# Residual layer norm: loads and stores through two on-chip rings of rows, a shorter pipeline, and one add in eight moved from TensorE to VectorE

## The chip, the cores and the metric

The kernel runs on one core of one Trainium2 chip. The metric is the device time of one execution in microseconds (us). The span of a profile, from the first to the last instruction, is 1.7 to 2.1 us shorter than the time of the same execution (3.2 us in one execution of dma_instr). Kernels are compared through their ratios to the kernel before (which was 251.4 to 251.7 us).

## The reference

```python
batch, seq, dim = 16, 1024, 512            # x and residual: float32, 33.5 MB each
z = x + residual
mean = np.mean(z, axis=-1, keepdims=True)
var = np.var(z, axis=-1, keepdims=True)
return (gamma * (z - mean) / np.sqrt(var + eps) + beta).astype(np.float32)
```

There are 16384 rows of 512 numbers. On the chip they are 128 "rows" j of 128x512 (one row per partition, 0.262 MB). For each, two inputs come in and one output goes out: 3 x 128 x 0.262 = 100.67 MB in all.

## The kernel before

Rows arrive in chunks of mostly 8, through two pools of buffers. TensorE adds z = x + residual into PSUM, the memory that its matmuls write, by two matmuls with the identity; ScalarE copies the sum back and totals it, then squares and totals; VectorE finishes. The stages of one group of 4 rows are spread over four steps.

```python
CHUNKS = [2, 2, 4] + [8] * 14 + [4, 2, 2]
GROUP = 4
STORE_LAG = 5          # in chunks
Z_BUFS = 7
R_BUFS = 4
# ... cut ...
    def g_add(g):                                   # TensorE
        # ... cut ...
        for j in range(j0, j0 + n):
            nc.tensor.matmul(ps, ident, Z[c][:, j, :], start=True, stop=False)
            nc.tensor.matmul(ps, ident, R[c][:, j, :], start=False, stop=True)
# ... cut: act_step = copy with a sum, square with a sum, sqrt (ScalarE);
#     affine1 = (z - mean) * gamma, affine2 = z * rstd + beta (VectorE, in place) ...
        for t in range(n_groups + 3):
            if ok(t) is not None:
                g_add(t)
            act_step(ok(t), ok(t - 1), ok(t - 2))   # copy t, square t-1, sqrt t-2
            if ok(t - 2) is not None:
                affine1(t - 2)
            if ok(t) is not None:
                negmean(t)
            if ok(t - 3) is not None:
                affine2(t - 3)
# ... cut ...
    for k in range(n_chunks + STORE_LAG):           # all on the sync engine's queue
        if k < n_chunks:
            load(k)
        c = k - STORE_LAG
        if c >= 0:
            while done <= c:
                done = next(steps)
            store(c)
```

## Time and profile before

| | before |
|---|---|
| time, median of 3 | 251.33 us (251.07 to 251.74) |
| span of the profile | 249.7 us |
| TensorE busy; its last matmul ends | 226.2 us; 229.3 us |
| VectorE busy; ends | 182.7 us; 246.0 us |
| DMA rate, 10 to 220 us | 428 GB/s |

Lines of the page of the kernel before: busy time of each engine, then the DMA engines' busy tenths and GB/s in 40 slices of 6.2 us, the DMA queues, and the chain of work that ended last, by engine.

```profile
PE 226.2 (91%) x516; PEld 99.2 (40%) x516; DVE 182.7 (73%) x328; ACT 180.4 (72%) x548; POOL 0.7 (0%) x6
...
DMA  6999999999999999999999999999999999987087
GB/s 245 421 440 428 425 429 379 438 427 425 436 430 430 429 433 425 428 433 433 428 428 430 425 433 425 433 425 433 428 432 427 428 430 416 427 353 299 42 357 315
...
q1 hardware_dynamic: 8640, 100.67, 95.4%
q8 instruction: 4, 0.07, 0.1%
q14 instruction: 8, 0.07, 0.1%
...
PE 88%; DVE 8%; DMA 1%; issue 1%; ACT 0%; DVEq 0%
```

The chain of waits is 88% TensorE, so TensorE looks like the limit. But the rate line stands between 416 and 440 GB/s in every slice from the 2nd to the 35th but one (379), so the DMA is full too. Both are close to their limit. The last five slices are what matters: 353, 299, 42, 357, 315.

The costliest groups (busy us, mean ns of one | idle us before) and the end in windows of 10 us (busy us and count per engine, granted TensorE clock, DMA share, GB/s):

```profile
L112 PE MATMUL ps<-z,ident 128*128 128x512 f32 x256 | 132.4, 599 | 0.0
...
L176 DVE SCALAR_TENSOR_TENSOR z<-z,nm,gamma_t 128x512 f32<-128x512 f32 x128 | 87.7, 745 | 1.1 <-ACT junk L139 1.1
```

```profile
core 0: us, PE busy (x) PEld busy (x) DVE busy (x) ACT busy (x) POOL busy (x), PEclk, DMA share, GB/s
...
210.00:220.00 10.00, 10.00 (x24) 4.39 (x24) 8.77 (x16) 8.66 (x29) 0.00 (x0) 1.00 1.03 433
220.00:230.00 10.00, 9.30 (x22) 3.80 (x20) 8.73 (x18) 8.66 (x27) 0.00 (x0) 1.00 0.68 287
230.00:240.00 10.00, 0.00 (x0) 0.00 (x0) 9.93 (x18) 4.98 (x17) 0.00 (x0) 0.68 0.37 157
240.00:250.00 10.00, 0.00 (x0) 0.00 (x0) 5.88 (x11) 0.00 (x0) 0.00 (x0) 0.50 0.82 341
```

A row has four matmul records (two matmuls, two records each) whose starts lie 0.43 us apart; 128 x 1.72 = 220 us. Up to 220 us the DMA share is 1. Then the loads are over, only stores of rows still being normalised are left, and the share falls to 0.68 and 0.37: the DMA engines wait for VectorE, which ends at 246.0 us.

### The profile page before, as it was taken

The page shows a single profiled execution, that of the slowest core. Times are in us where ns is not written, and L with a number is a line of the kernel's source. Part 1 is how long each engine was busy: PE and PEld are TensorE (multiplying, and loading weights), DVE is VectorE, ACT ScalarE, POOL GpSimd, SP SyncE. Part 2 cuts the span into 40 slices and gives each one's busy share as a digit, 9 for nine tenths or more (in the row PEclk, how much of TensorE's full clock was granted, in tenths as well). Part 3 has the DMA queues.
Part 4 walks back from the last instruction along what each step waited for, and adds up shares of the span by engine and source line. Part 5 has one row for each costly group of instructions (what it writes and reads, how often), then busy time and mean ns, then how long its engine had stood idle before and what let it go on. Part 6 is the DMA issues. An engine that isn't in the chain of part 4 may idle for free.

```text
span 249.7 us, 2117 instructions
## 1 busy us (share of the span) xinstructions
PE 226.2 (91%) x516; PEld 99.2 (40%) x516; DVE 182.7 (73%) x328; ACT 180.4 (72%) x548; POOL 0.7 (0%) x6
## 2 busy tenths in 40 slices
PE   5999999999999999999999999999999999997000
PEld 1444444444444444444444444444444444442000
DVE  1121266888888888898888888888988888889993
ACT  2157578888777777788887777777888877779600
POOL 1000000000000000000000000000000000000000
PEclk9999999999999999999999999999999999999755
DMA  6999999999999999999999999999999999987087
GB/s 245 421 440 428 425 429 379 438 427 425 436 430 430 429 433 425 428 433 433 428 428 430 425 433 425 433 425 433 428 432 427 428 430 416 427 353 299 42 357 315
DMA packets 8656, 100.80 MB, mean 404 GB/s; under 512 B 962, under 2 KB 962, under 8 KB 2500
## 3 DMA queue, kind: packets, MB, share of 16 engines
q1 hardware_dynamic: 8640, 100.67, 95.4%
q8 instruction: 4, 0.07, 0.1%
q14 instruction: 8, 0.07, 0.1%
q10 hardware_dynamic: 4, 0.00, 0.0%
HBM read 67.11 MB, written 33.55 MB: 403 GB/s over the span
## 4 chain that ended last, share of the span: by engine, by line
PE 88%; DVE 8%; DMA 1%; issue 1%; ACT 0%; DVEq 0%
PE ps L112 43%; PE ps L113 43%; DVE z L191 5%; DVE z L176 3%; PE ps L98 1%; DMA gb_row<-in_gamma_dram 1%; ACT z L121 0%; DVEq L267 0%; DVE rstd L188 0%; DVE nm L163 0%
## 5 line engine op out<-in xcount | busy, mean ns | idle before, releaser
L112 PE MATMUL ps<-z,ident 128*128 128x512 f32 x256 | 132.4, 599 | 0.0
L113 PE MATMUL ps<-r,ident 128*128 128x512 f32 x256 | 131.7, 596 | 0.0
L121 ACT ACTIVATE z<-ps 128x512 f32<-128x512 f32 x128 | 75.4, 589 | 50.2 <-PE ps L113 50.2
L139 ACT ACTIVATE junk<-z,nm 128x512 f32<-128x512 f32 x128 | 90.5, 711 | 1.4 <-DVE nm L163 1.4
L191 DVE SCALAR_TENSOR_TENSOR z<-z,rstd,beta_t 128x512 f32<-128x512 f32 x128 | 87.8, 747 | 1.2
L176 DVE SCALAR_TENSOR_TENSOR z<-z,nm,gamma_t 128x512 f32<-128x512 f32 x128 | 87.7, 745 | 1.1 <-ACT junk L139 1.1
L112 PEld LDWEIGHTS ps<-z,ident 128*128 128x128 f32 x256 | 49.1, 192 | 62.8 <-issue 48.7
L113 PEld LDWEIGHTS ps<-r,ident 128*128 128x128 f32 x256 | 49.0, 192 | 62.3 <-issue 61.7
L163 DVE TENSOR_SCALAR nm<-sm 128x4 f32<-128x4 f32 (+1 forms) x34 | 5.8, 170 | 54.9 <-ACT z L121 54.9
L121 ACT ACTIVATION_READ_ACCUMULATOR z<-ps 128x1 f32 x128 | 24.9, 195 | 0.0
L139 ACT ACTIVATION_READ_ACCUMULATOR junk<-z,nm 128x1 f32 x128 | 24.4, 191 | 0.0
L151 ACT ACTIVATE std<-ssq,eps_t 128x4 f32<-128x4 f32 (+1 forms) x34 | 9.8, 289 | 0.1
L98 PE MATMUL ps<-gb_row,ones 1*128 1x512 f32 x4 | 3.7, 1085 | 3.1 <-DMA gb_row<-in_gamma_dram 3.1
L188 DVE RECIPROCAL rstd<-std 128x4 f32<-128x4 f32 (+1 forms) x34 | 5.8, 170 | 0.0
L121 ACT ACT_TABLE_LOAD x1 | 1.3, 1283 | 4.3 <-DMA z<-in_x_dram 4.3
L99 DVE COPY gamma_t<-ps 128x512 f32<-128x512 f32 x1 | 0.7, 692 | 4.2 <-PE ps L98 4.2
L98 PEld LDWEIGHTS ps<-gb_row,ones 1*128 1x128 f32 x4 | 1.1, 307 | 4.2 <-issue 3.3
L99 DVE COPY beta_t<-ps 128x512 f32<-128x512 f32 x1 | 0.7, 692 | 1.0 <-PE ps L98 1.0
L151 ACT ACT_TABLE_LOAD x1 | 1.3, 1283 | 0.0
L87 DVE MEMSET ones<- 1x128 f32 x1 | 0.2, 165 | 0.8 <-PEq L253 0.8
masks.py:199 POOL TENSOR_SCALAR_AFFINE_SELECT ident<-ident 128x128 f32<-128x128 f32 x1 | 0.3, 295 | 0.1
masks.py:197 POOL MEMSET ident<- 128x128 f32 x1 | 0.2, 205 | 0.3 <-POOLq L253 0.3
(5 smaller groups left out, 0.5 us busy)
## 6 DMA issues: line engine op xcount, KB each, us to landing
z<-in_x_dram SPq DMA_DIRECT2D x14, 2048.0 KB, 19.4
r<-in_residual_dram SPq DMA_DIRECT2D x14, 2048.0 KB, 23.9
out_dram<-z SPq DMA_DIRECT2D x14, 2048.0 KB, 26.6
z<-in_x_dram SPq DMA_DIRECT2D x4, 512.0 KB, 7.4
r<-in_residual_dram SPq DMA_DIRECT2D x4, 512.0 KB, 8.2
z<-in_x_dram SPq DMA_DIRECT2D x2, 1024.0 KB, 9.0
r<-in_residual_dram SPq DMA_DIRECT2D x2, 1024.0 KB, 15.0
out_dram<-z SPq DMA_DIRECT2D x4, 512.0 KB, 8.3
```

Of the source, the lines that this page charges most:

```text
L87: nc.vector.memset(ones, 1.0)
L98: nc.tensor.matmul(ps, ones, gb_row[:, k, :], start=True, stop=True)
L99: nc.vector.tensor_copy(dest, ps)
L112: nc.tensor.matmul(ps, ident, Z[c][:, j, :], start=True, stop=False)
L113: nc.tensor.matmul(ps, ident, R[c][:, j, :], start=False, stop=True)
L121: nc.scalar.activation(out=Z[c][:, j0 + k, :], in_=PS[g_copy][k], func=ACT.Identity, accum_out=sm[:, k : k + 1],)
L139: nc.scalar.activation(out=junk, in_=Z[c][:, j0 + k, :], func=ACT.Square, bias=NM[g_square][:, k : k + 1], accum_out=ssq[:, k : k + 1],)
L151: nc.scalar.activation(out=std[:, :n], in_=SSQ.pop(g)[:, :n], func=ACT.Sqrt, bias=eps_t[:, 0:1], scale=inv_d,)
L163: nc.vector.tensor_scalar(out=nm[:, :n], in0=NM[g][:, :n], scalar1=-inv_d, scalar2=None, op0=ALU.mult,)
L176: nc.vector.scalar_tensor_tensor(out=zj, in0=zj, scalar=NM[g][:, k : k + 1], in1=gamma_t, op0=ALU.add, op1=ALU.mult,)
L188: nc.vector.reciprocal(out=rstd[:, :n], in_=STD.pop(g)[:, :n])
L191: nc.vector.scalar_tensor_tensor(out=zj, in0=zj, scalar=rstd[:, k : k + 1], in1=beta_t, op0=ALU.mult, op1=ALU.add,)
```

## The change

Its intent is to let loads run further ahead, to move larger pieces, to shorten the pipeline, and to take work off TensorE. The two pools become two rings of 64 and 32 rows; loads are 2 MB from the first one on (the last two of each input 1 MB); stores are 4 MB (the last three smaller), asked for when the loads are at least 40 rows ahead; every eighth row is added on VectorE; the pipeline has three steps. Below, R stands for the rings with their chunk sizes, P for the three-step pipeline, V for the vector adds.

```diff
-CHUNKS = [2, 2, 4] + [8] * 14 + [4, 2, 2]
+X_CHUNKS = [8] * 15 + [4, 4]
+R_CHUNKS = [8] * 15 + [4, 4]
+OUT_CHUNKS = [16] * 7 + [8, 4, 4]
 GROUP = 4
-STORE_LAG = 5
-Z_BUFS = 7
-R_BUFS = 4
+Z_ROWS = 64
+R_ROWS = 32
+STORE_LAG = 40
+ADD_PERIOD = 8
 # ... cut: pools replaced by two tiles addressed modulo their rows ...
+    def add_on_vector(g):
+        # ... cut ...
+        for j in range(j0, j0 + n):
+            if on_vector(j):                       # j % ADD_PERIOD == ADD_PERIOD - 1
+                nc.vector.scalar_tensor_tensor(
+                    out=zrow(j), in0=zrow(j), scalar=0.0, in1=rrow(j),
+                    op0=ALU.add, op1=ALU.add,
+                    accum_out=SM[g][:, j - j0 : j - j0 + 1])
 # ... cut ...
+        stages = [
+            (0, add),
+            (0, copy_then_sqrt),
+            (1, square),
+            (2, affine2),
+            (0, add_on_vector),
+            (1, affine1),
+            (0, negmean),
+        ]
+        for t in range(n_groups + 2):
 # ... cut ...
+    for lo, n in spans(X_CHUNKS):
+        asked = lo + n
+        load_x(lo, n)
+        while loads_r and loads_r[0][0] + loads_r[0][1] <= asked:
+            while added < loads_r[0][0] + loads_r[0][1] - R_ROWS:
+                added, done = next(steps)
+            load_r(*loads_r.pop(0))
+        store_due()        # stores whose rows end at or before asked - STORE_LAG
```

More of the change, by code (lines that the diff above doesn't have):

```diff
@@ L40, with spans, dram @@
     inv_d = 1.0 / float(D)
-    assert N == P * sum(CHUNKS)
-    NJ = max(CHUNKS)
-    starts = [P * sum(CHUNKS[:c]) for c in range(len(CHUNKS))]
-    def rows(t, c):
-        return t[starts[c] : starts[c] + P * CHUNKS[c], :].rearrange(
-            "(p j) d -> p (j d)", p=P
-        )
+    total = N // P
+    def spans(sizes):
+        assert sum(sizes) == total
+        return [(sum(sizes[:c]), n) for c, n in enumerate(sizes)]
+    blocks = spans(OUT_CHUNKS)
+    def dram(t, lo, n):
+        b0, bn = next(b for b in blocks if b[0] <= lo and lo + n <= b[0] + b[1])
+        v = t[P * b0 : P * (b0 + bn), :].rearrange("(p j) d -> p j d", p=P)
+        return v[:, lo - b0 : lo - b0 + n, :].rearrange("p a b -> p (a b)")
     consts = ctx.enter_context(tc.tile_pool(name="consts", bufs=1))
-    zpool = ctx.enter_context(tc.tile_pool(name="zpool", bufs=Z_BUFS))
-    rpool = ctx.enter_context(tc.tile_pool(name="rpool", bufs=R_BUFS))
     small = ctx.enter_context(tc.tile_pool(name="small", bufs=6))
@@ L58, with part, load_x, load_r @@
     ctx.enter_context(tc.manual_schedule())
-    Z, R = {}, {}
-    def load(c):
-        n = CHUNKS[c]
-        z = zpool.tile([P, NJ, D], FP32, tag="z", name="z")
-        r = rpool.tile([P, NJ, D], FP32, tag="r", name="r")
-        nc.sync.dma_start(
-            out=z[:, :n, :].rearrange("p a b -> p (a b)"), in_=rows(xf, c)
-        )
-        nc.sync.dma_start(
-            out=r[:, :n, :].rearrange("p a b -> p (a b)"), in_=rows(rf, c)
-        )
-        Z[c], R[c] = z, r
-    def store(c):
-        n = CHUNKS[c]
-        z = Z.pop(c)
-        nc.sync.dma_start(
-            out=rows(of, c), in_=z[:, :n, :].rearrange("p a b -> p (a b)")
-        )
+    zbuf = consts.tile([P, Z_ROWS, D], FP32)
+    rbuf = consts.tile([P, R_ROWS, D], FP32)
+    def part(buf, size, lo, n):
+        assert lo % size + n <= size
+        return buf[:, lo % size : lo % size + n, :].rearrange("p a b -> p (a b)")
+    def load_x(lo, n):
+        nc.sync.dma_start(out=part(zbuf, Z_ROWS, lo, n), in_=dram(xf, lo, n))
+    def load_r(lo, n):
+        nc.sync.dma_start(out=part(rbuf, R_ROWS, lo, n), in_=dram(rf, lo, n))
+    def store(lo, n):
+        nc.sync.dma_start(out=dram(of, lo, n), in_=part(zbuf, Z_ROWS, lo, n))
+    def zrow(j):
+        return zbuf[:, j % Z_ROWS, :]
+    def rrow(j):
+        return rbuf[:, j % R_ROWS, :]
+    def on_vector(j):
+        return j % ADD_PERIOD == ADD_PERIOD - 1
     gb_row = consts.tile([1, 2, D], FP32)
@@ L101, with add @@
     groups = []
-    for c, n in enumerate(CHUNKS):
+    for lo, n in spans(R_CHUNKS):
         for j in range(0, n, GROUP):
-            groups.append((c, j, min(GROUP, n - j)))
-    PS, NM, SSQ, STD = {}, {}, {}, {}
-    def g_add(g):
-        c, j0, n = groups[g]
-        PS[g] = []
+            groups.append((lo + j, min(GROUP, n - j)))
+    n_groups = len(groups)
+    PS, SM, NM, SSQ, STD = {}, {}, {}, {}, {}
+    def add(g):
+        j0, n = groups[g]
+        SM[g] = small.tile([P, GROUP], FP32, tag="sm", name="sm")
@@ L110, in g_add @@
         for j in range(j0, j0 + n):
+            if on_vector(j):
+                continue
             ps = psum.tile([P, D], FP32, tag="ps", name="ps")
-            nc.tensor.matmul(ps, ident, Z[c][:, j, :], start=True, stop=False)
-            nc.tensor.matmul(ps, ident, R[c][:, j, :], start=False, stop=True)
-            PS[g].append(ps)
-    def act_step(g_copy, g_square, g_sqrt):
-        if g_copy is not None:
-            c, j0, n = groups[g_copy]
-            sm = small.tile([P, GROUP], FP32, tag="sm", name="sm")
-            for k in range(n):
+            nc.tensor.matmul(ps, ident, zrow(j), start=True, stop=False)
@@ new lines, in add @@
+            nc.tensor.matmul(ps, ident, rrow(j), start=False, stop=True)
+            PS[j] = ps
+    def add_on_vector(g):
+        j0, n = groups[g]
+        for j in range(j0, j0 + n):
+            if on_vector(j):
+                nc.vector.scalar_tensor_tensor(
+                    out=zrow(j),
+                    in0=zrow(j),
+                    scalar=0.0,
+                    in1=rrow(j),
+                    op0=ALU.add,
+                    op1=ALU.add,
+                    accum_out=SM[g][:, j - j0 : j - j0 + 1],
+                )
@@ L121, in act_step, with copy_then_sqrt @@
+    def copy_then_sqrt(g):
+        j0, n = groups[g] if g < n_groups else (0, 0)
+        before = g - 2 if g >= 2 else None
+        for j in range(j0, j0 + n):
+            if j in PS:
                 nc.scalar.activation(
-                    out=Z[c][:, j0 + k, :],
-                    in_=PS[g_copy][k],
+                    out=zrow(j),
+                    in_=PS.pop(j),
                     func=ACT.Identity,
-                    accum_out=sm[:, k : k + 1],
+                    accum_out=SM[g][:, j - j0 : j - j0 + 1],
@@ L126, in act_step @@
                 )
-                if k == 0 and g_sqrt is not None:
-                    sqrt(g_sqrt)
-                    g_sqrt = None
-            NM[g_copy] = sm
-            PS.pop(g_copy)
-        if g_sqrt is not None:
-            sqrt(g_sqrt)
-        if g_square is not None:
-            c, j0, n = groups[g_square]
-            ssq = small.tile([P, GROUP], FP32, tag="ssq", name="ssq")
-            for k in range(n):
-                junk = junkp.tile([P, D], FP32, tag="junk", name="junk")
-                nc.scalar.activation(
-                    out=junk,
-                    in_=Z[c][:, j0 + k, :],
-                    func=ACT.Square,
-                    bias=NM[g_square][:, k : k + 1],
-                    accum_out=ssq[:, k : k + 1],
-                )
-            SSQ[g_square] = ssq
+                if before is not None:
+                    sqrt(before)
+                    before = None
@@ new lines, in copy_then_sqrt, with negmean, square @@
+        if before is not None:
+            sqrt(before)
+    def negmean(g):
+        n = groups[g][1]
+        nm = small.tile([P, GROUP], FP32, tag="nm", name="nm")
+        nc.vector.tensor_scalar(
+            out=nm[:, :n],
+            in0=SM.pop(g)[:, :n],
+            scalar1=-inv_d,
+            scalar2=None,
+            op0=ALU.mult,
+        )
+        NM[g] = nm
+    def square(g):
+        j0, n = groups[g]
+        ssq = small.tile([P, GROUP], FP32, tag="ssq", name="ssq")
+        for k in range(n):
+            junk = junkp.tile([P, D], FP32, tag="junk", name="junk")
+            nc.scalar.activation(
+                out=junk,
+                in_=zrow(j0 + k),
+                func=ACT.Square,
+                bias=NM[g][:, k : k + 1],
+                accum_out=ssq[:, k : k + 1],
+            )
+        SSQ[g] = ssq
@@ L148, in sqrt @@
     def sqrt(g):
-        n = groups[g][2]
+        n = groups[g][1]
         std = small.tile([P, GROUP], FP32, tag="std", name="std")
@@ L158, in sqrt @@
         STD[g] = std
-    def negmean(g):
-        n = groups[g][2]
-        nm = small.tile([P, GROUP], FP32, tag="nm", name="nm")
-        nc.vector.tensor_scalar(
-            out=nm[:, :n],
-            in0=NM[g][:, :n],
-            scalar1=-inv_d,
-            scalar2=None,
-            op0=ALU.mult,
-        )
-        NM[g] = nm
     def affine1(g):
-        c, j0, n = groups[g]
+        j0, n = groups[g]
         for k in range(n):
-            zj = Z[c][:, j0 + k, :]
             nc.vector.scalar_tensor_tensor(
-                out=zj,
-                in0=zj,
+                out=zrow(j0 + k),
+                in0=zrow(j0 + k),
                 scalar=NM[g][:, k : k + 1],
@@ L183, in affine1 @@
             )
+        NM.pop(g)
     def affine2(g):
-        c, j0, n = groups[g]
+        j0, n = groups[g]
         rstd = small.tile([P, GROUP], FP32, tag="rstd", name="rstd")
@@ L189, in affine2 @@
         for k in range(n):
-            zj = Z[c][:, j0 + k, :]
             nc.vector.scalar_tensor_tensor(
-                out=zj,
-                in0=zj,
+                out=zrow(j0 + k),
+                in0=zrow(j0 + k),
                 scalar=rstd[:, k : k + 1],
@@ L198, in affine2 @@
             )
-        NM.pop(g)
-    n_groups = len(groups)
-    def ok(g):
-        return g if 0 <= g < n_groups else None
     def compute_steps():
-        done = 0
-        for t in range(n_groups + 3):
-            if ok(t) is not None:
-                g_add(t)
-            act_step(ok(t), ok(t - 1), ok(t - 2))
-            if ok(t - 2) is not None:
-                affine1(t - 2)
-            if ok(t) is not None:
-                negmean(t)
-            if ok(t - 3) is not None:
-                affine2(t - 3)
-                c, j0, n = groups[t - 3]
-                if j0 + n == CHUNKS[c]:
-                    done = c + 1
-            yield done
@@ L224 @@
-    steps = compute_steps()
-    done = 0
-    n_chunks = len(CHUNKS)
-    for k in range(n_chunks + STORE_LAG):
-        if k < n_chunks:
-            load(k)
-        if k == 0:
-            spread()
-        c = k - STORE_LAG
-        if c >= 0:
-            while done <= c:
-                done = next(steps)
-            store(c)
+        stages = [
[7 more added lines that the diff above has]
+        ]
@@ new lines, in compute_steps @@
+        added = done = 0
+        for t in range(n_groups + 2):
+            for lag, stage in stages:
+                if 0 <= t - lag < n_groups or stage is copy_then_sqrt:
+                    stage(t - lag)
+            if t < n_groups:
+                added += groups[t][1]
+            if t >= 2:
+                done += groups[t - 2][1]
+            yield added, done
+    steps = compute_steps()
+    added = done = asked = 0
+    loads_r = spans(R_CHUNKS)
+    stores = spans(OUT_CHUNKS)
@@ new lines, in store_due @@
+    def store_due():
+        nonlocal added, done
+        while stores and (
+            stores[0][0] + stores[0][1] <= asked - STORE_LAG or asked == total
+        ):
+            lo, n = stores.pop(0)
+            while done < lo + n:
+                added, done = next(steps)
+            store(lo, n)
+    for lo, n in spans(X_CHUNKS):
+        asked = lo + n
+        assert not stores or stores[0][0] >= asked - Z_ROWS
+        load_x(lo, n)
+        while loads_r and loads_r[0][0] + loads_r[0][1] <= asked:
+            while added < loads_r[0][0] + loads_r[0][1] - R_ROWS:
+                added, done = next(steps)
+            load_r(*loads_r.pop(0))
+        if lo == 0:
+            spread()
+        store_due()
```

## The prediction

> **What bounds the kernel now.** Two things almost tie. (a) DMA: the 10 us windows show the DMA engines' busy share at 0.99 to 1.03 from 10 to 220 us, at about 429 GB/s, so 100.67 MB need 100.67/0.429 = 235 us. The Trainium skill, "DMA: Bandwidth & Descriptors", section "Where 436 GB/s comes from", puts the fabric's ceiling at 435; the trace agrees. (b) TensorE: the timeline shows 4 matmul records 0.43 us apart per row, so 128 x 1.72 = 220 us; the chain of waits is 86% these two lines. TensorE ends at 222.5 us with VectorE behind it; in the last three windows the DMA share falls to 0.68, 0.37, 0.82, because the last chunks are still being normalised and only their stores are left. That tail of about 7 MB takes 30 us where 16 would do. It is the loss to win back.
>
> **What the change does.**
> - VectorE takes 16 of 128 adds. TensorE falls to 112 x 1.72 = 192 us; ScalarE loses 16 copies (16 x 0.78, 12 us).
> - VectorE gains 16 three-operand instructions with a sum; estimate 0.7 to 0.9 us each, from the 0.69 us between starts of the present ones: 183 becomes about 195. Per group of 4: 8 x 0.69 + 0.34 + 0.4 = 6.3 us, 1.6 us per row.
> - DMA moves the same bytes, 1.83 us per row (0.786 MB), so every engine is now faster per row than DMA.
> - Loads run up to 56 rows before the first store. The x load that reuses a stored row waits for that store to land, but 4 MB of loads are still queued behind the store (10 us), so the queue should not run dry.
> - At the end 48 rows of stores (12.6 MB, 29 us) stand behind the last load. My sum: last load lands near 207 us, last row finished near 223, its store reached by the queue near 234: 10 us of slack.
>
> **Critical path.** Of the removed TensorE time nearly nothing counts by itself; it lets compute finish under the DMA. The chain should become DMA throughout: 235 us, plus 2.8 us lost at the start (the first window moved 3.07 MB instead of 4.29), plus 1 to 2 us for the last store's landing: span 239; time minus span was 1.6 us before. Predicted 240.5 us, a gain of about 4.3%. Range 238.5 to 244.5. Chances: faster by over 2% 0.92, within 2% 0.07, slower 0.01.
>
> **What would show each step.** DMA share about 1.0 in every window from 10 us to the end, at 425 to 432 GB/s; no hole after 220 us. TensorE busy about 195 us, idle time released by loads. VectorE busy 193 to 200 us, finished by about 225 us. The last stores wait little for VectorE. The new vector adds under 1 us each.
>
> **What would make it wrong.** Pure stores at the end slower than mixed traffic (bytes over busy share in before's tail gives about 420 GB/s, 0.6 us only). Loads of 16 KB out of 32 KB pitch, or 4 MB stores, moving slower; or an uneven engine that leaves others idle at the waits for a store. VectorE behind by over 10 us: its chain with ScalarE within a step may stall so that a group takes over 7 us. TensorE's clock falling in its new gaps (the Trainium skill, "TensorE: Matmul & The Clock Gate", Part 1; before shows it granted 0.50 after the last matmul): a few us, inside the slack.

## The result, and the profile after

The changed kernel took 242.98 us (median of 4 runs, 242.69 to 243.06), and the kernel before 251.54 us beside it. The ratio is 0.966 with a 95% interval of 0.9641 to 0.9678. Such a ratio is the mean time of one kernel's runs over that of the other's of the same rounds, so it is not quite the ratio of the medians.

The same lines of the changed kernel's page:

```profile
PE 203.2 (84%) x452; PEld 87.6 (36%) x452; DVE 192.7 (80%) x356; ACT 169.8 (70%) x514; POOL 0.7 (0%) x6
...
DMA  7999999999999999999999999999999999999993
GB/s 262 435 435 435 430 422 419 423 432 431 435 443 432 400 428 432 430 430 430 431 432 443 426 419 427 427 468 405 419 432 430 450 401 419 443 435 435 427 413 160
...
q1 hardware_dynamic: 6336, 100.67, 98.1%
q8 instruction: 3, 0.05, 0.1%
q14 instruction: 7, 0.06, 0.1%
...
DVE 53%; DMA 19%; PE 17%; issue 3%; ACT 3%; SPq 1%; DVEq 0%
```

The DMA queue's own share rose from 95.4% of 249.7 us to 98.1% of 241.0 us. Both are 236 to 238 us of work: the transfers did not get faster, the holes went. The chain is no longer TensorE; it now runs mostly through VectorE, which was to prove misleading.

```profile
L132 PE MATMUL ps<-zbuf,ident 128*128 128x512 f32 x224 | 117.6, 607 | 0.0
...
L140 DVE SCALAR_TENSOR_TENSOR zbuf<-zbuf,rbuf 128x512 f32<-128x512 f32 x16 | 11.0, 685 | 0.0
```

```profile
core 0: us, PE busy (x) PEld busy (x) DVE busy (x) ACT busy (x) POOL busy (x), PEclk, DMA share, GB/s
...
210.00:220.00 10.00, 7.37 (x18) 2.95 (x16) 8.82 (x15) 8.12 (x24) 0.00 (x0) 1.00 1.00 430
220.00:230.00 10.00, 0.00 (x0) 0.00 (x0) 9.93 (x20) 4.44 (x14) 0.00 (x0) 0.51 0.97 419
230.00:240.00 10.00, 0.00 (x0) 0.00 (x0) 1.22 (x2) 0.00 (x0) 0.00 (x0) 0.50 0.70 298
240.00:250.00 10.00, 0.00 (x0) 0.00 (x0) 0.00 (x0) 0.00 (x0) 0.00 (x0) 0.84 0.01 2
```

There is no hole between 220 and 230 us (share 0.97 instead of 0.68). A vector add takes 0.685 us. VectorE ends at 231.2 us (the last window shows it busy for 1.22 us), the last matmul at 217.4 us. The queue's timeline (start, duration, issue) shows how late the last stores were issued:

```profile
175.89 0.33 SPq L84 DMA_DIRECT2D rbuf<-in_residual_dram  x1
180.78 50.80 SPq L87 DMA_DIRECT2D out_dram<-zbuf  x5
```

The last five stores were issued between 180.8 and 231.6 us. The last four were held by VectorE (44.3 us of waiting in the queue's waits), and yet the DMA engines had work nearly all the time: the share is 0.97 from 220 to 230 us.

The sum of my prediction, with the measured terms: 100.67 MB at 429 GB/s is 234.7 us (the windows from 10 to 230 us give 94.5 MB in 220 us, 429). The start lost 2.3 us (the first 10 us moved 3.31 MB instead of 4.29; I had 2.8). Time minus span was 2.0 us (I had 1.6). The rest of the span, 241.0 - 234.7 - 2.3 = 4.0 us, is the end, where I had 1 to 2. So two questions are left: which part of the change made the gain, and what are the 2 to 3 us at the end?

### The profile page after: what moved, and what is told of

It reads as the page before. It is cut to its first block, busy times and chain, and to the rows that moved or that the text cites. A ratio compares the mean times of both kernels' runs of the same rounds, so it can differ in the third digit from the quotient of the medians.

```text
span 241.0 us, 1990 instructions
## 1 busy us (share of the span) xinstructions
PE 203.2 (84%) x452; PEld 87.6 (36%) x452; DVE 192.7 (80%) x356; ACT 169.8 (70%) x514; POOL 0.7 (0%) x6
## 3 DMA queue, kind: packets, MB, share of 16 engines
q1 hardware_dynamic: 6336, 100.67, 98.1%
## 4 chain that ended last, share of the span: by engine, by line
DVE 53%; DMA 19%; PE 17%; issue 3%; ACT 3%; SPq 1%; DVEq 0%
DVE zbuf L209 26%; DVE zbuf L224 23%; DMA rbuf<-in_residual_dram 19%; PE ps L133 9%; PE ps L132 8%; DVE zbuf L140 3%; ACT junk L185 1%; DVE rstd L222 1%; ACT zbuf L156 1%; DVE nm L171 1%; ACT L197 1%; SPq L81 0%; DVEq L312 0%; SPq L87 0%; ACT std L197 0%
## 5 line engine op out<-in xcount | busy, mean ns | idle before, releaser
L133 PE MATMUL ps<-rbuf,ident 128*128 128x512 f32 x224 | 117.5, 607 | 9.4 <-DVE zbuf L209 6.4
L132 PE MATMUL ps<-zbuf,ident 128*128 128x512 f32 x224 | 117.6, 607 | 0.0
L209 DVE SCALAR_TENSOR_TENSOR zbuf<-zbuf,nm,gamma_t 128x512 f32<-128x512 f32 x128 | 89.5, 749 | 12.8 <-ACT junk L185 12.8
L156 ACT ACTIVATE zbuf<-ps 128x512 f32<-128x512 f32 x112 | 66.0, 589 | 46.6 <-PE ps L133 46.5
L185 ACT ACTIVATE junk<-zbuf,nm 128x512 f32<-128x512 f32 x128 | 90.4, 711 | 1.6 <-DVE nm L171 1.6
L224 DVE SCALAR_TENSOR_TENSOR zbuf<-zbuf,rstd,beta_t 128x512 f32<-128x512 f32 x128 | 87.7, 747 | 1.1
L133 PEld LDWEIGHTS ps<-rbuf,ident 128*128 128x128 f32 x224 | 43.0, 194 | 66.4 <-issue 53.0
L132 PEld LDWEIGHTS ps<-zbuf,ident 128*128 128x128 f32 x224 | 43.6, 195 | 56.3 <-issue 43.3
L185 ACT ACTIVATION_READ_ACCUMULATOR junk<-zbuf,nm 128x1 f32 x128 | 24.3, 190 | 0.0
L156 ACT ACTIVATION_READ_ACCUMULATOR zbuf<-ps 128x1 f32 x112 | 21.8, 195 | 0.0
```

What stands on the lines that cost most here:

```text
L132: nc.tensor.matmul(ps, ident, zrow(j), start=True, stop=False)
L133: nc.tensor.matmul(ps, ident, rrow(j), start=False, stop=True)
L156: nc.scalar.activation(out=zrow(j), in_=PS.pop(j), func=ACT.Identity, accum_out=SM[g][:, j - j0 : j - j0 + 1],)
L185: nc.scalar.activation(out=junk, in_=zrow(j0 + k), func=ACT.Square, bias=NM[g][:, k : k + 1], accum_out=ssq[:, k : k + 1],)
L209: nc.vector.scalar_tensor_tensor(out=zrow(j0 + k), in0=zrow(j0 + k), scalar=NM[g][:, k : k + 1], in1=gamma_t, op0=ALU.add, op1=ALU.mult,)
L224: nc.vector.scalar_tensor_tensor(out=zrow(j0 + k), in0=zrow(j0 + k), scalar=rstd[:, k : k + 1], in1=beta_t, op0=ALU.mult, op1=ALU.add,)
```

## The experiments

### Which part made the gain

The three parts make eight combinations; the kernel before has none of them and the changed kernel all three. The other six were run. Theory 1 is that of the prediction: the DMA is the limit, and compute has to end under it, which needs TensorE relieved and a queue of stores long enough to cover the drain. Theory 2: the long drain of four steps was the whole loss. Theory 3: the rings and larger transfers feed the DMA better.

**P alone** (f_p), in the kernel before:

```diff
-        for t in range(n_groups + 3):
+        for t in range(n_groups + 2):
-            affine1(t - 2); negmean(t); affine2(t - 3)
+            affine2(t - 2); affine1(t - 1); negmean(t)
 # ... cut: the conditions around each call, and the counting of finished chunks ...
```

> The kernel before with only the order of the pipeline changed to three steps (all adds stay on TensorE, the old pools, chunks and stores). Theory 1 (TensorE is the limit until about 229 us, and the stores' slack decides the tail): TensorE still ends near 229 us, VectorE ends near 240 instead of 246, time 245 to 248 us. Theory 2 (the long drain of four steps was the whole loss): as fast as the full change, 242 to 244 us. Theory 3 (only the rings and the larger transfers help): 250 to 252 us.

**V alone** (f_v), in the kernel before: rows with j % 8 == 7 skip the matmuls and the copy, and

```diff
             affine1(t - 2)
+            add_on_vector(t)
             negmean(t)
```

> The kernel before with only one row in eight added on VectorE. Theory 1: TensorE no longer limits (busy about 200 us), loads are limited by DMA alone, the drain of four steps stays: 243 to 247 us. Theory 2 (drain): 249 to 252 us. Theory 3 (rings): 250 to 252 us.

**V and P** (f_vp), both edits, pools and chunks of before:

> The kernel before with the vector adds and the three-step pipeline, but its own pools, chunks and stores. Theory 1: 241 to 244 us, within 1% of the full change, DMA share near 1.0 to about 230 us. Theory 3 (rings needed): 246 us or more.

**V and R** (f_vr), in the changed kernel:

```diff
-            (2, affine2), (0, add_on_vector), (1, affine1), (0, negmean),
+            (2, affine1), (0, add_on_vector), (0, negmean), (3, affine2),
 # ... cut: one step more in the loop ...
```

> The changed kernel with the old four-step pipeline. VectorE should end about 6 us later, near 237 us instead of 231. Theory 1: the last 1 MB store then goes out after the queue has run dry: 245 to 248 us. If the queue's slack hides it: 243 us.

**P and R** (f_pr), in the changed kernel:

```diff
-ADD_PERIOD = 8
+ADD_PERIOD = 1000
```

> The changed kernel (rings, large transfers, three steps) with all adds left on TensorE. Theory 1 (compute must end under the DMA; the rings do nothing for TensorE): TensorE starts 5 us later than in the kernel before[...], ends near 236 us, VectorE near 247, time 250 to 255 us, so no gain at all over before. Theory 3 (the rings and large transfers are worth something by themselves): under 246 us, below the three-step change alone (246.7).

**R alone** (f_r), the edits of f_vr and f_pr together:

> The changed kernel's rings and large transfers alone: all adds on TensorE, the old four steps. Theory 1: slower than before, 255 to 261 us. Theory 3: 251 us or less.

Measured (all six correct; the two ends are read from the timelines of the profiles):

| parts | time, median us | ratio to before (95%) | last matmul ends, us | VectorE ends, us |
|---|---|---|---|---|
| none (before) | 251.3 | 1 | 229.3 | 246.0 |
| P (f_p) | 246.68 | 0.9805 (0.979 to 0.9819) | 229.4 | 241.1 |
| V (f_v) | 246.48 | 0.9809 (0.9768 to 0.9851) | 223.7 | 240.7 |
| V, P (f_vp) | 243.65 | 0.9685 (0.9671 to 0.9699) | 222.4 | 234.4 |
| R (f_r) | 258.94 | 1.0307 (1.0283 to 1.0332) | 234.2 | 251.9 |
| P, R (f_pr) | 253.98 | 1.0117 (1.0085 to 1.0149) | 233.7 | 246.5 |
| V, R (f_vr) | 243.29 | 0.9678 (0.9653 to 0.9703) | 217.4 | 236.3 |
| V, P, R (after) | 242.98 | 0.966 (0.9641 to 0.9678) | 217.4 | 231.2 |

Theory 3 falls: the rings by themselves cost 3%, and with the shorter pipeline still 1%. Their first loads are 2 MB instead of 0.5 MB, so the first matmul that reads a residual row starts at 12.9 us instead of 8.7, and with all the adds on TensorE its last matmul ends 4.9 us later than before. That is most of the 7.3 us that the span grew; of the rest, VectorE ends another 1.0 us later after TensorE, and the last store, 1 MB instead of 0.5, ends the span 5.1 us after VectorE instead of 3.7. Their stores of 16 rows wait for the last of them (the queue's waits of f_r give 102 us of stores waiting for VectorE, those of the kernel before 70): the window of f_r from 220 to 230 us (columns as above) shows 10 us in which nothing moved at all, with TensorE busy all through it.

```profile
220.00:230.00 10.00, 10.00 (x25) 4.44 (x24) 7.54 (x16) 8.15 (x25) 0.00 (x0) 1.00 0.00 0
```

Theory 2 falls as well: the shorter pipeline alone gains 1.95%, the vector adds alone 1.91%, and the two together, on the old pools, 3.15% of the full change's 3.4%. (By the 2% rule of the record both single parts are "unclear", but both intervals lie wholly below 1.) Theory 1 had five of the six ranges right. The vector adds are what makes the rings harmless: they turn 1.0117 into 0.966. With V in place, P and R gain about the same. My reading is that both let VectorE's last rows be covered, P by ending sooner (234.4 us instead of 240.7), R by a longer queue of stores; no run shows this for R, whose parts (ring depth, size of loads and stores, the lag of the stores) were not run one by one. Adding the second of them to the first brings 0.2 to 0.3%, which these intervals do not separate from nothing.

The miss of theory 1 is f_vr: VectorE ended 5 us later than in the changed kernel, and the DMA share did fall, but the time was only 0.3 us longer, where I had expected 2 to 5. (The expectation's other branch named 243 us, but for a queue that hides the late rows; the share below shows that it did not.)

```profile
220.00:230.00 10.00, 0.00 (x0) 0.00 (x0) 9.96 (x17) 4.33 (x14) 0.00 (x0) 0.57 0.82 354
230.00:240.00 10.00, 0.00 (x0) 0.00 (x0) 6.21 (x11) 0.00 (x0) 0.00 (x0) 0.50 0.88 367
```

A hole of 0.18 x 10 us did not cost 1.8 us. Something in the changed kernel's own end must take as long as that hole.

### What the end of the changed kernel waits for

Theory A: the 16 DMA engines drift apart by themselves, and the slowest sets the end. Theory B: VectorE's last rows are too late.

**Transfers alone** (dma_only), the result wrong:

```diff
             for lag, stage in stages:
-                if 0 <= t - lag < n_groups or stage is copy_then_sqrt:
-                    stage(t - lag)
+                pass
```

> Wrong result on purpose: the same loads and stores in the same order with the row computation taken out, so stores wait for loads only. Theory A (the last 2.5 us over my prediction are the spread of the 16 DMA engines' ends plus the landing): 242 to 243.3 us, with the DMA share falling gradually over the last 3 us. Theory B (they are VectorE's late last rows): 239.5 to 241.2 us.

**VectorE ends early** (early_tail), the result wrong:

```diff
         nc.vector.reciprocal(out=rstd[:, :n], in_=STD.pop(g)[:, :n])
+        if g >= n_groups - 4:
+            return
```

> Wrong result on purpose: the changed kernel without the second affine step on the last four groups, so VectorE ends near 220 us instead of 231 and the last store is queued about 10 us earlier. Theory A: no change, 242.3 to 243.3 us. Theory B: 240 to 241.5 us.

Measured: dma_only 240.24 us (240.22 to 240.32, ratio 0.956), early_tail 243.17 us (242.84 to 243.3, ratio 0.9674), though VectorE now ended at 225.9 us (5 us sooner; I had expected 11, but VectorE then waited for ScalarE). So dma_only lies in the range of theory B and early_tail in that of theory A, and neither theory can hold. Theory B falls by early_tail. Theory A falls by dma_only: the transfers do not drift apart on their own. So the computing adds 2.7 us to the transfers (242.98 against 240.24; by the ratios, 0.966 and 0.956, 2.5 us) without VectorE's last rows being what it waits for. The windows at the end show where, first the changed kernel, then the transfers alone (the same columns, without ScalarE's, which did nothing there):

```profile
core 0: us, PE busy (x) PEld busy (x) DVE busy (x) ACT busy (x) POOL busy (x), PEclk, DMA share, GB/s
...
236.00:238.00 2.00, 0.00 (x0) 0.00 (x0) 0.00 (x0) 0.00 (x0) 0.00 (x0) 0.50 0.50 209
238.00:240.00 2.00, 0.00 (x0) 0.00 (x0) 0.00 (x0) 0.00 (x0) 0.00 (x0) 0.50 0.10 41
```

```profile
236.00:238.00 2.00, 0.00 (x0) 0.00 (x0) 0.00 (x0) 0.00 (x0) 1.00 0.34 143
238.00:240.00 2.00, 0.00 (x0) 0.00 (x0) 0.00 (x0) 0.00 (x0) 1.00 0.00 0
```

In the changed kernel the DMA engines run out one after another between 236 and 240 us; alone they all stop before 238. The trace also records each DMA packet. An engine works on one at a time, so the records can be strung into 16 chains, each next packet put where the one before ended. (In the kernels that compute, a chain is not always certain in the middle, but where the 16 chains end is.) Their ends, in us from the first data packet:

```
before       246.5 x8  246.6 x8
f_vr         237.9 x5  238.0 x9  238.1 x2
dma_only     234.8 x2  234.9 x2  235.0 x2  235.1 x3  235.2 x3  235.3 x2  235.4 x2
after        234.6 to 235.0 x10  236.3  236.4  236.7  237.0  237.4  237.8
early_tail   234.6 to 235.0 x9   236.2  236.3  236.3  236.4  237.0  237.3  238.1
dma_traffic  234.7 to 235.4 x15  236.2
dma_instr    234.6 to 235.1 x10  235.7  236.0  236.6  236.7  237.5  237.9
dma_instr2   234.6 to 235.0 x6   236.3 to 237.3 x8   240.1  240.2
```

In all of these the span ends 3.0 to 3.3 us after the last chain does (part of it is the time before the first packet). Six engines of the changed kernel are 1 to 3 us late. In before and in f_vr all end together, because there the last store reaches engines that have been idle. That answers f_vr: its hole is filled while the late engines catch up, and both kernels end within 0.3 us of each other. The packet records of f_vr show it: nine engines ran out of work at 225.0 to 225.5 us and three at 226.6, all twelve took up again at 227.0 to 227.2 (on the time axis of the list above), and four did not stop there at all.

What makes single engines late? The queue part of the pages gives a candidate. The changed kernel has 10 packets of "instruction", that is of fetched program code, on two queues (shown above), the transfers alone have none:

```profile
q1 hardware_dynamic: 6336, 100.67, 99.1%
q10 hardware_dynamic: 4, 0.00, 0.0%
```

Theory D: fetching the instructions takes turns with the data on some of the DMA engines. The Trainium skill, "CRC Debugging", lists queue 14 as that of the instruction refills, and "DMA: Bandwidth & Descriptors", section "Queues, rings and completion order", says that an engine goes round the queues that have work for it, one packet at a time; whether the trace agrees is what the next runs test. Theory E, the rival: the compute engines' reads and writes of the on-chip memory slow some DMA engines.

**The instructions without the traffic** (dma_instr), the result wrong: the changed kernel with the rows replaced by rows of 4 elements in a small buffer of their own, so that as many instructions are issued but they neither touch nor await a transfer.

```diff
     def zrow(j):
-        return zbuf[:, j % Z_ROWS, :]
+        return zs[:, j % Z_ROWS, :]        # zs: 128 x 64 x 4; rrow likewise
```

> Wrong result on purpose: the loads and stores of the changed kernel, and as many instructions on each engine as it has (about 1990), but each on rows of 4 elements of a small buffer of their own that no transfer touches. Theory D (fetching the instructions takes turns with the data on some of the DMA engines, and the slowest engine ends the kernel): 242.2 to 243.3 us, as the changed kernel, with the DMA share falling gradually over the last 3 us. Theory E (the compute engines' traffic to the on-chip memory slows some DMA engines): 240.1 to 240.6 us, as the transfers alone.

**Twice the instructions** (dma_instr2), the same with the list of groups doubled:

```diff
+    groups = groups + [(lo + total, n) for lo, n in groups]
```

> Wrong result on purpose: the same with every instruction of the small rows issued twice over, about 3900. Theory D: 2 to 3 us more than with them once, 244.5 to 246 us, if the second half's fetches fall on the same DMA engines; about 243 to 244 if they fall on others. Theory E: 240.1 to 240.6 us.

**The traffic without the instructions** (dma_traffic), the result wrong:

```diff
-GROUP = 4
+GROUP = 8
-            (0, add), (0, copy_then_sqrt), (1, square), (2, affine2), ...
+            (2, half), (2, act), (1, vec), (1, act), (0, vec_r), (0, act),
+            # vec: z = max(z + 0, z) on 128x4096; half: on 128x2048; vec_r: z + r
+            # act: Identity, z to z, on 128x4096
```

> Wrong result on purpose: the same transfers, with VectorE and ScalarE kept busy on the real rows (about 170 us each, mostly 128x4096 in place) by under 100 instructions, TensorE unused. Theory D: 240.1 to 240.7 us, all DMA engines ending together. Theory E: 241.5 us or more.

Measured: dma_instr 243.21 us (242.64 to 244.05, ratio 0.9679), dma_instr2 245.19 us (244.98 to 245.57, ratio 0.9755), dma_traffic 241.31 us (241.02 to 241.5, ratio 0.9598). The end of dma_instr looks like that of the changed kernel, and its instruction packets are about as many (11, of which one has 48 bytes and ten have 8 or 16 KB, as in the changed kernel; then 21 in dma_instr2):

```profile
236.00:238.00 2.00, 0.00 (x0) 0.00 (x0) 0.00 (x0) 0.00 (x0) 0.00 (x0) 1.00 0.46 193
238.00:240.00 2.00, 0.00 (x0) 0.00 (x0) 0.00 (x0) 0.00 (x0) 0.00 (x0) 1.00 0.10 41
```

```profile
q8 instruction: 3, 0.05, 0.1%
q14 instruction: 8, 0.06, 0.1%
```

```profile
q8 instruction: 7, 0.11, 0.2%
q14 instruction: 14, 0.11, 0.1%
```

So the instructions alone, on a buffer of 4 elements per row, cost all that the real computing costs, and doubling them costs another 2.0 us. The traffic run lies between the two theories' ranges, 1 us above the transfers alone (0.956 to 0.9598, 0.38% of 251.4 us). Its page explains it:

```profile
PE 4.1 (2%) x4; PEld 1.0 (0%) x4; DVE 177.7 (74%) x55; ACT 173.5 (73%) x52; POOL 0.7 (0%) x6
...
q1 hardware_dynamic: 6336, 100.67, 98.8%
q14 instruction: 1, 0.01, 0.0%
```

It had one instruction fetch left, and exactly one DMA engine ended late, at 236.2 us. In this run the chains show 15 engines without a gap of 0.1 us after the start, and one with a gap of 0.30 us, just while the fetch ran (at 181 us), after which its next packet of 16 KB took 1.27 us instead of 0.61. That is 0.30 + 0.66 = 0.96 us lost by one 8 KB fetch, and the kernel was about as much longer: 0.96 us by the ratios (whose intervals leave some 0.6 us either way), 1.07 by the medians, 0.7 between the profiled spans. The other 15 engines, under 178 us of VectorE and 174 us of ScalarE traffic, ended as in the transfers alone, so theory E falls for these two engines. TensorE's traffic was not in that run; but dma_instr, which has no traffic of full rows on any engine, leaves nothing for it to explain.

The same can be counted in every one of these runs. A gap is a time of over 0.1 us, from 5 us after the first data packet on, in which one of the 16 chains has no data packet; "late" are engines that end after 235.5 us; the last column adds the ends of all 16 engines and subtracts the same sum of the transfers alone.

| run | fetches of 8 or 16 KB during the transfers | gaps | late engines | sum of the 16 ends, us more |
|---|---|---|---|---|
| dma_only | 0 | 0 | 0 | 0 |
| dma_traffic | 1 | 1 | 1 | 0.9 |
| after | 10 | 10 | 6 | 8.2 |
| dma_instr | 10 | 10 | 6 | 7.1 |
| early_tail | 11 | 11 | 7 | 9.3 |
| dma_instr2 | 21 | 21 | 10 | 19.7 |

Every gap ends within 0.1 us of the end of a fetch, and the engines together lose 0.7 to 0.9 us per fetch. So the trace agrees with the page: a data packet waits while a fetch takes its turn. Spread evenly, 8.2 us would be 0.5 us for each engine; it costs the kernel 2.5 to 2.7 us because nearly all of it falls on six, and the slowest ends the kernel. Theory D is shown.

### An attempt to have fewer instructions

With D, the instructions of TensorE (904 of 1990 in the profile) look worth removing. GpSimd is idle and can add four rows in one instruction.

```diff
-                nc.tensor.matmul(...)   # two per row; every eighth row on VectorE
+        nc.gpsimd.tensor_tensor(out=z, in0=z, in1=r, op=ALU.add)   # 128 x 2048
-                    out=zrow(j), in_=PS.pop(j),
+                    out=PS.pop(j), in_=zrow(j),                     # ScalarE, for the sum
```

> The changed kernel with all adds on GpSimd, four rows in one 128x2048 instruction (its 2048-element add is estimated at 4.5 us from the Trainium skill's GPSIMD Engine Reference, under the 7.3 us that the transfers of four rows need), ScalarE summing from the result. About 1100 instructions, none on TensorE. Theory D: 241.8 to 242.9 us, since TensorE's fetches[...] are gone and ScalarE's and VectorE's stay. Theory E: no better than 242.9. If GpSimd and VectorE hinder each other: 245 us or more.

Measured: correct, 335.71 us, ratio 1.3354. The add took 4.74 us on average (4.49 to 5.09), near the 4.5 of the Trainium skill's "GPSIMD Engine Reference", section 3.1, but it held VectorE up. VectorE's and GpSimd's timelines (start, duration):

```profile
57.54 4.98 DVE L223 SCALAR_TENSOR_TENSOR zbuf<-zbuf,rstd,beta_t 128x512 f32<-128x512 f32 x1
62.44 4.98 DVE L208 SCALAR_TENSOR_TENSOR zbuf<-zbuf,nm,gamma_t 128x512 f32<-128x512 f32 x1
```

```profile
57.03 4.94 POOL L129 TENSOR_TENSOR zbuf<-zbuf,rbuf 128x2048 f32<-128x2048 f32 x1
62.30 9.47 POOL L129 TENSOR_TENSOR zbuf<-zbuf,rbuf 128x2048 f32<-128x2048 f32 x2 [0.33 <-DMA rbuf<-in_residual_dram]
```

A VectorE instruction that takes 0.75 us otherwise takes 4.98 when it meets an add of 4.94 us; this befell 26 of the 256, and VectorE's busy time rose from 192.7 to 305.5 us. The Trainium skill, "SBUF — State Buffer", section "Who interferes with whom", says of it that a VectorE instruction with two inputs in the on-chip memory contends with a GpSimd instruction that reads it, and calls the ports that the two share an exclusive lock; the trace agrees. I had not looked there before the run. At 335.71 us the run says nothing on theory D. It was the only attempt; what is left to the transfers alone is 2.7 us.

## Why the prediction was right or wrong, point by point

- **The limit and the gain: right.** I predicted 240.5 us, from a DMA that is never idle between its start and its end; the transfers alone take 240.24. The changed kernel took 242.98, inside the range of 238.5 to 244.5; the gain was 3.4%, not 4.3%. The share was 0.95 to 1.07 in every window from 10 to 230 us, at 429 GB/s on average; 425 to 432 in each window was too narrow, it was 408 to 451. "To the end" did not hold: from 230 to 240 us the share was 0.70.
- **"TensorE ends at 222.5 us" was a misreading.** That is where the chain of waits leaves TensorE; its last matmul ended at 229.3 us.
- **TensorE's busy time** was 203.2 us, not about 195. It started at half its rate: the timeline's matmul records lie 0.86 us apart until 19 us, then 0.43. Its last matmul ended 13.8 us before VectorE, so I take it to have cost nothing; no run tests that.
- **VectorE**: 192.7 us busy against 193 to 200, the adds 0.685 us against 0.7 to 0.9. It ended at 231.2 us instead of near 223. "The last stores wait little for VectorE" was wrong, they waited for it to the end, so the 10 us of slack were not there: the last store was issued at 231.2 us, as VectorE ended. That this cost nothing is shown by early_tail (5 us sooner changed nothing), but f_vr (5 us later) already leaves a hole.
- **The step that failed** is the last term of the sum, "plus 1 to 2 us for the last store's landing". The end took 4.0 us. The landing itself was small: the same sum for dma_only, whose span is 238.5 us, leaves 1.5 us (2.0 with that run's own rate of 430 GB/s). The missing 2.5 us (2.7 by the medians) are the instruction fetches, which make some of the DMA engines late by 1 to 3 us (dma_instr, dma_instr2). I had named "an uneven engine that leaves others idle" as a risk, but at the waits for a store, not at the end, and without its cause.
- **"Of the removed TensorE time nearly nothing counts by itself"**: too strong. V alone is worth 1.9%, and without it the rings make the kernel slower (1.0117). "It lets compute finish under the DMA" is what was seen.

## What to carry to other kernels

When two engines are near their limit, look at the end of the profile: here the work that was left after TensorE and the loads had ended was what could be won, and a shorter drain, a longer queue of stores, and less load on the other engine were partly substitutes for one another. Larger transfers and deeper rings were not a gain in themselves where the DMA was already full; here they delayed the first row and the last store, and cost 3% alone. This kernel, which keeps all 16 DMA engines full to the end, also pays 2.5 to 2.7 us for the fetching of its own instructions, because it ends with the slowest engine: compare such a kernel with its transfers alone, and count its instruction packets.

## What the Trainium skill lacked or had wrong

- "Runtime: NRT & Kernel Launch", section "Instruction fetch mechanics", calls the cost of crossing a 16 KiB block of instructions one DMA tail-bump, mostly hidden. In these kernels, whose DMA is full, it is not hidden: 1934 instructions cost 3.0 us (243.21 us with them against 240.24 without), and 3806 cost 5.0.
- No page says what one fetch costs the transfers beside it: an 8 KB one held up one DMA engine by 0.96 us (a gap of 0.30 us, then a 16 KB packet of 1.27 us instead of 0.61), and over all the runs a fetch of 8 or 16 KB cost the 16 engines together 0.7 to 0.9 us.
- "CRC Debugging" names queue 14 only for the refills; here they came on queues 8 and 14, the former in packets of 16 KB and the latter of 8 KB. Queue 8's are missing in dma_traffic and f_pool, where TensorE has only 4 matmuls.
- "DMA: Bandwidth & Descriptors", section "Where 436 GB/s comes from", says that about 358 GB/s binds transfers between HBM (the chip's main memory) and the on-chip memory, without saying when. Just above, the same page gives that figure as the share of a core when both cores of a pair stream, and 425 GB/s for a core alone; this core, running alone, moved 429 GB/s, loads and stores mixed, for 220 us. So the figure is not wrong, but the sentence lacks its condition.
